# A two-layer decoder step: zero matmuls around the norms, and finer steps in the recurrent branch and the retention output

## The chip, the cores and the metric

One core of a Trainium2 chip. Times are device microseconds of the kernel's execution on that core, in several runs; the profile is that of one execution. TensorE (PE) multiplies, PEld is its weight load, VectorE is DVE, ScalarE is ACT, GpSimd is POOL, and SyncE (SP) issues most DMAs.

## What is computed

Two layers over 256 prompt tokens and 8 x 8 sample tokens (320 in all), model width 1024, f32. Cut to what matters:

```python
for l in range(DEPTH):                                   # DEPTH = 2
    xn = rmsnorm(x, norm1_g[l])
    q, k, v, g_ret, xr, g_rnn, ga, gb = split(xn @ w_in[l])
    o = groupnorm(retention(rotary(q), rotary(k), v, r0[l]))
    ret_out = (silu(g_ret) * o) @ w_ret_out[l]
    xc = conv_b + sum(xcat[:, w:w + t] * cw[w] for w in range(4))      # causal, 4 taps
    r, i = sigmoid(xc @ wa + ba), sigmoid(xc @ wx + bx)                # 16 blocks of 64
    a = exp(-8 * r * softplus(-lam))
    h = scan(a, sqrt(1 - a * a) * i * xc, h0)                          # h_t = a_t h_(t-1) + u_t
    rnn_out = (h * gelu(g_rnn)) @ w_rnn_out[l]
    x = x + (sigmoid(ga) * ret_out + sigmoid(gb) * rnn_out) @ w_o[l]
    x = x + peer(rmsnorm(x, norm2_g[l]), ...)            # top-16 of 128 x 128 experts, 8 heads
y = rmsnorm(x, normf_g)
```

## The kernel before

**Blocks.** All weights of a layer's projections are cut into blocks of 128x1024 (512 KB). `run` (line 222) executes them in a fixed order, one after the other on TensorE. In a layer, counted from 0: 0 to 7 q and k, 8 to 15 v, 16 to 23 `g_ret`, 24 to 31 `xr`, 32 to 39 `g_rnn`, 40 to 47 `ga`, 48 to 55 `gb`, then the two output projections in turn, `w_o`, and the query weights of the expert stage; behind these the expert stage runs its own phases. For f32 accuracy every product is made of three matmuls, so activations and weights are kept as a high and a low part: a block against 320 tokens is 24 matmuls of 320 columns. The blocks 0 and 1 run as one interleaved pair.

**Weight splits.** At the start of block k, `run` calls `split(k + 2)` (its high half is a cast on ScalarE, line 217; its low half a subtraction on VectorE, line 219, or on GpSimd where the block's `lo` says so) and issues the load of block k + 5 on SP. High and low halves have three buffers each.

**Background.** Retention, the recurrent branch (`rglru`) and others are Python generators. `run` advances them by half a block's budget twice in each block, in the middle and at its end; each `yield x` costs x of the budget. The numbers behind `yield` therefore fix at which half block each step's instructions are put into the engines' queues. ScalarE, VectorE and GpSimd execute their queues in order.

**Norms.** `norm_T` (line 157), called before block 0 (`norm1`) and before the query weights (`norm2`) in each layer: squares of x (line 140 on ScalarE, 142 on VectorE; in the first norm here, in the others by the code that made x), the factor r by `rstd` (lines 148 to 154), 24 transposes of x on TensorE into the eight PSUM banks (line 174; x[2] holds the sample tokens and goes first), six matmuls that spread r over partitions (line 178), its copy R, then in eight parts y = x g R (line 191, VectorE), its high part `xh` (193, ScalarE) and its low part `xl` (196, VectorE for parts 0, 3 and 6, else GpSimd). The pair's first matmul (336) waits for the first `xh`. Behind the query pair stand the score matmuls (881), whose keys an SP transfer (872) brings into a pool that is opened after the norm's own is closed.

**Retention output.** Behind retention, `o` is multiplied by the gate in two halves of 1280 elements (671), each cast to `rin_h` (672), with the low parts `rin_l` (678) one step behind.

**Recurrent branch** (`rglru`). For each of 8 channel blocks: `conv(c)` on VectorE (one line 713 and three of line 715), as soon as enough `xr` blocks are done; two gates (728: two f32 matmuls each of 344 columns; 729, tanh on ScalarE) and 731. The convolution runs two blocks ahead of the gates. Then exp (738), Dt in halves (739), one square root over all (741), the state in halves (745 to 748) with eight scans (751), and the branch's output in halves (766, 770, cast 771, low part 772). `bg.drain()` before the first output block forces what is left.

Of the kernel before, what the change touches and what calls it, by code (L numbers as in the profile page):

```python
# [10 lines left out]
F32 = mybir.dt.float32  # L11
F32R = mybir.dt.float32r
F16 = mybir.dt.float16
# [4 lines left out]
OP = mybir.AluOpType  # L18
# [68 lines left out]
class Trunk:  # L87
# [23 lines left out]
    def consts(self):  # L111
        nc, a = self.nc, self.a
        self.ident = self.cp.tile([128, 128], F32, name="ident")
        self.iota_a = self.cp.tile([128, 128, 2], F16, name="iota_a")
        self.gt = self.cp.tile([128, self.depth, 2, 8], F32, name="gt")
        self.eps = self.cp.tile([128, 1], F32, name="eps")
        nc.vector.memset(self.eps, EPS)
        self.nk = self.cp.tile([128, 4, 3], F32, name="nk")
        nc.vector.memset(self.nk, 1.0)
        self.warm()  # L120
        self.x = [self.cp.tile([128, D], F32, name=f"x{t}") for t in range(3)]
        nc.sync.dma_start(self.x[2][:NST], a["x_sample"].rearrange("b t d -> (b t) d"))
        nc.sync.dma_start(self.ident, a["c_ident"])
        for t in range(2):
            nc.sync.dma_start(self.x[t], a["x_prompt"][0, t * 128:(t + 1) * 128, :])
        nc.sync.dma_start(self.gt, a["gt"])
# [18 lines left out]
    def rstd(self, c=slice(0, 3)):  # L145
# [8 lines left out]
        nc.vector.scalar_tensor_tensor(r, w, 1.5, r, op0=OP.add, op1=OP.mult)  # L154
        return self.nk[:, 2, :]

    def norm_T(self, l, which, first=False):
        nc = self.nc
        np_ = self.open("np")
        if first:  # L160
            for k in range(RAWS):
                self.load(k)
            self.late_consts()
            for t in (2, 0, 1):
                for h in range(2):
                    self.square(t, h, np_.tile([128, 512], F32, tag="junk", name="junk", bufs=2), eng=("act", "dve")[h])
        r = self.rstd()
        if first:
            self.split(0)
        ps = [self.bank("acc") for _ in range(4)] + [self.bank("m") for _ in range(2)] + [self.bank("h") for _ in range(2)]  # L170
        for t in (2, 0, 1):
            r0, n = TOK[t]
            for c in range(8):
                nc.tensor.transpose(ps[c][:, r0:r0 + n], self.x[t][:n, c * 128:(c + 1) * 128], self.ident[:n, :n])
        at = {0: (6, NT), 1: (7, NT), 2: (7, NT + 128)}
        for t, (r0, n) in enumerate(TOK):
            b, o = at[t]
            nc.tensor.matmul(ps[b][:, o:o + n], r[:n, t:t + 1].to_broadcast([n, 128]), self.ident[:n, :n], start=True,
                             stop=True, skip_group_check=True)
        R = np_.tile([128, NT], F32, name="R")  # L180
        nc.scalar.copy(R[:, :128], ps[6][:, NT:NT + 128])
        nc.vector.tensor_copy(R[:, 128:], ps[7][:, NT:NT + 192])
        if first:
            self.split(1)
        self.xh = self.cp.tile([128, 8, NT], F32R, tag="xh", name="xh")
        self.xl = self.cp.tile([128, 8, NT], F32R, tag="xl", name="xl")
        ys = {}
        for c in range(9):
            if c < 8:
                ys[c] = y = np_.tile([128, NT], F32, tag="y", name="y", bufs=8)  # L190
                nc.vector.scalar_tensor_tensor(y, ps[c][:, :NT], self.gt[:, l, which, c:c + 1], R, op0=OP.mult,
                                               op1=OP.mult)
                nc.scalar.copy(self.xh[:, c], y)
            if c:
                eng = nc.vector if c - 1 in (0, 3, 6) else nc.gpsimd
                eng.tensor_tensor(self.xl[:, c - 1], ys.pop(c - 1), self.xh[:, c - 1].bitcast(F32), op=OP.subtract)
        self.close("np")
# [24 lines left out]
    def run(self):  # L222
        self.items, self.blocks, self.raw, self.hl = [], [], {}, {}
        for l in range(self.depth):
            Layer(self, l).plan()
        self.credit = self.credit2 = 0.0
        for k, it in enumerate(self.items):
            self.k = k
            if it.get("pre"):
# [41 lines left out]
class Layer:  # L271
# [244 lines left out]
    def retention(self):  # L516
# [148 lines left out]
        while not self.sg_done:  # L665
            yield 0.5
        hi = mx.tile([128, 8, NT], F32R, tag="s3", name="rin_h")
        for j in range(3):
            s = slice(4 * j, 4 * j + 4)
            if j < 2:  # L670
                nc.vector.scalar_tensor_tensor(o[:, s], o[:, s], 0.5, self.sg[:, s], op0=OP.mult, op1=OP.mult)
                nc.scalar.copy(hi[:, s], o[:, s])
                yield 1.5
            if j == 1:
                lo = mx.tile([128, 8, NT], F32R, tag="s1", name="rin_l")
            if j:
                s = slice(4 * j - 4, 4 * j)
                nc.vector.tensor_tensor(lo[:, s], o[:, s], hi[:, s].bitcast(F32), op=OP.subtract)
                yield 1.5
        self.rin = (hi, lo)  # L680
        T.close("rt")
        rg = self.rg = T.open("rg")
# [13 lines left out]
    def rglru(self):  # L696
# [18 lines left out]
                nc.vector.scalar_tensor_tensor(B[:, c, :], A[:, c, w:w + OUTW], vec[:, c, 1 + w:2 + w], B[:, c, :],  # L715
                                               op0=OP.mult, op1=OP.add)

        for c in range(-2, 8):
            if c < 6:
                while self.xr_done < c + 3:  # L720
                    yield 0.5
                conv(c + 2)
            if c < 0:
                yield 1.8
                continue
            for g, dst in ((0, E), (1, Dt)):
                p = T.bank("m")
# [1 line left out]
                nc.scalar.activation(dst[:, c, :], p[:, :OUTW], AF.Tanh, bias=self.hb[:, c, g:g + 1],  # L729
                                     scale=0.5)  # L730
            nc.scalar.activation(C[:, c, :], E[:, c, :], AF.Tanh, bias=z5[:, c:c + 1], scale=z5[:, c:c + 1])
            yield 1.8
        for j in range(2):
            s = slice(4 * j, 4 * j + 4)
            while not self.ge_done:
                yield 0.5
            for c in range(4 * j, 4 * j + 4):
                nc.scalar.activation(E[:, c, :], E[:, c, :], AF.Exp, bias=z6[:, c:c + 1], scale=z6[:, c:c + 1])
            nc.vector.scalar_tensor_tensor(Dt[:, s], Dt[:, s], 1.0, B[:, s], op0=OP.add, op1=OP.mult)
            yield 3.0  # L740
        nc.scalar.activation(C, C, AF.Sqrt, scale=0.25)
        yield 3.5
        for j in range(2):
            s = slice(4 * j, 4 * j + 4)
            nc.vector.tensor_tensor(Dt[:, s], Dt[:, s], C[:, s], op=OP.mult)
            nc.vector.scalar_tensor_tensor(Dt[:, s], E[:, s], 1.0, Dt[:, s], op0=OP.add, op1=OP.mult)
            nc.vector.memset(E[:, s, SEG - 1::3 + DS], 0.0)
            nc.vector.tensor_copy(Dt[:, s, SEG - 1::3 + DS], self.h0[:, s, :])
            yield 3.0
            for c in range(4 * j, 4 * j + 4):  # L750
                nc.vector.tensor_tensor_scan(B[:, c, :], E[:, c, :], Dt[:, c, :], 0.0, op0=OP.mult, op1=OP.add)
                if c % 2:
                    yield 0.9
        nc.scalar.copy(rec[:, :, 9:12], A[:, :, SEG - 3:SEG])
        nc.scalar.copy(rec[:, :, 12:36].rearrange("p c (b w) -> p c b w", w=3), seg[:, :, :, DS:DS + 3])
        nc.scalar.copy(rec[:, :, 0:1], B[:, :, NPT - 1:NPT])
# [4 lines left out]
        ge = self.ge  # L761
        hi = rg.tile([128, 8, NT], F32R, tag="C", name="hin_h")
        lo = rg.tile([128, 8, NT], F32R, tag="D", name="hin_l")
        for j in range(2):
            s = slice(4 * j, 4 * j + 4)
            nc.vector.tensor_tensor(ge[:, s, :NPT], ge[:, s, :NPT], B[:, s, :NPT], op=OP.mult)
            for c in range(4 * j, 4 * j + 4):
                bs = bass_seg(B[:, c, :])
                gs = ge[:, c, NPT:].rearrange("p (b t) -> p b t", t=DS)
                nc.vector.tensor_tensor(gs, gs, bs, op=OP.mult)  # L770
            nc.scalar.copy(hi[:, s], ge[:, s])
            nc.vector.tensor_tensor(lo[:, s], ge[:, s], hi[:, s].bitcast(F32), op=OP.subtract)
            yield 3.0
        self.hin = (hi, lo)

    def post_rnn(self, c):
# [648 lines left out]
```

## Time and profile before

| | |
|---|---|
| runs (us) | 2508.48, 2512.42, 2505.75; median 2508.48 |
| profiled execution | 2508.14, of which the span from the first to the last instruction is 2506.4 |
| mean granted TensorE clock | 0.985 |
| busy share of the span | PE 97%, PEld 87%, DVE 78%, ACT 44%, POOL 19% |
| matmuls | 16556 |
| idle of TensorE for a weight's low half | 12.6 + 8.4 us in its two longest groups |

A busy share is an average over stages with different limits: TensorE is never far from full, so what is to be read is where it waits, and at which clock it goes on afterwards. In the rows, the number in square brackets is the idle time of the engine ahead of the row and what ended it; the granted clock is given as a share of 2.4 GHz. A layer takes some 1250 us; times are counted from the span's start, and the second layer's first norm lies near 1250.

### The profile page before, as it was taken

The numbers are of one execution on the slowest core, as the hardware profiler recorded it, in microseconds if no ns is written. First come the engines' busy times: TensorE is split into PE (matmuls) and PEld (weight loads), VectorE is DVE, ScalarE is ACT, GpSimd is POOL, SyncE is SP. The second block draws the span as 40 slices with busy tenths as digits, with TensorE's granted clock in tenths as the row PEclk, the third lists the DMA queues.
The fourth block names the chain that finished last, engine by engine and source line by source line (L and its number), as shares of the span: only waits on it lengthen the run. The fifth ranks groups of instructions, "written<-read, shape, count | busy, mean of one in ns | idle before, by whom it ended". The sixth has DMA issues, their size and how long they took to land. (4 is left out here: it accounts for less than half of the span.)

```text
span 2506.4 us, 42676 instructions
## 1 busy us (share of the span) xinstructions
PE 2419.1 (97%) x16556; PEld 2175.8 (87%) x16556; DVE 1943.1 (78%) x3491; ACT 1092.6 (44%) x1539; POOL 485.4 (19%) x305
## 2 busy tenths in 40 slices
PE   8999999999999999999999899999998999999998
PEld 7879898999898897688788798999998988976886
DVE  7465657888788878989864656578887988788897
ACT  4336434455334443244544373444543344432444
POOL 0000003100102541145300000041001035411453
PEclk9999999999999999999999899999999999999999
DMA  6333444456867998899752334444568689988996
GB/s 235 117 110 118 130 151 130 149 177 227 306 202 275 355 352 303 289 335 355 287 206 89 109 113 142 143 132 156 184 233 294 203 295 351 350 309 291 328 356 238
DMA packets 174507, 571.67 MB, mean 228 GB/s; under 512 B 20832, under 2 KB 28000, under 8 KB 173536
## 3 DMA queue, kind: packets, MB, share of 16 engines
q1 hardware_dynamic: 135568, 427.54, 50.1%
q0 software_dynamic: 36864, 134.23, 14.0%
q10 hardware_dynamic: 1872, 7.16, 0.8%
q8 instruction: 130, 2.13, 0.3%
q14 instruction: 73, 0.60, 0.1%
HBM read 545.76 MB, written 23.10 MB: 227 GB/s over the span
## 5 line engine op out<-in xcount | busy, mean ns | idle before, releaser
L217 ACT CAST hi<-raw 128x1024 fp32r<-128x1024 f32 x684 | 717.0, 1049 | 686.9 <-PE ps_acc L1199 393.4
L219 DVE TENSOR_TENSOR lo<-raw,hi 128x1024 fp32r<-128x1024 f32 x660 | 803.2, 1221 | 270.1 <-ACT hi L217 267.2
L945 PE MATMUL ps_h<-xh,lo 128*128 128x256 f32 x2048 | 582.8, 285 | 12.6 <-DVE lo L219 12.6
L943 PE MATMUL ps_h<-xh,hi 128*128 128x256 f32 x2048 | 587.8, 287 | 0.0
L944 PE MATMUL ps_h<-xl,hi 128*128 128x256 f32 x2048 | 581.6, 284 | 0.0
L945 PEld LDWEIGHTS ps_h<-xh,lo 128*128 128x128 f32 x2048 | 395.1, 193 | 14.7 <-DVE lo L219 14.5
L944 PEld LDWEIGHTS ps_h<-xl,hi 128*128 128x128 f32 x2048 | 395.5, 193 | 0.1
L943 PEld LDWEIGHTS ps_h<-xh,hi 128*128 128x128 f32 x2048 | 395.3, 193 | 0.1
L1197 PE MATMUL ps_acc<-hi,hh 128*128 128x512 f32 x944 | 373.8, 396 | 0.0
L1198 PE MATMUL ps_acc<-lo,hh 128*128 128x512 f32 x944 | 368.4, 390 | 2.7 <-DVE lo L219 2.7
L1199 PE MATMUL ps_acc<-hi,hl 128*128 128x512 f32 x944 | 369.0, 391 | 0.7
L1243 POOL DMA_INDIRECT g<-in_peer_u,eS x128 | 203.4, 1589 | 781.8 <-DVE g L1252 490.1
L356 PE MATMUL ps_acc<-xh,hi 128*128 128x320 f32 x960 | 310.6, 324 | 3.0 <-ACT hi L217 3.0
L358 PE MATMUL ps_acc<-xh,lo 128*128 128x320 f32 x960 | 301.8, 314 | 8.4 <-DVE lo L219 8.4
L357 PE MATMUL ps_acc<-xl,hi 128*128 128x320 f32 x960 | 300.4, 313 | 0.0
L1243 POOL DMA_INDIRECT g<-in_peer_v,eS x128 | 203.0, 1586 | 349.5 <-DVE xs L1266 286.9
L1198 PEld LDWEIGHTS ps_acc<-lo,hh 128*128 128x128 f32 x944 | 177.4, 188 | 41.7 <-DVE lo L219 5.3
L1199 PEld LDWEIGHTS ps_acc<-hi,hl 128*128 128x128 f32 x944 | 177.2, 188 | 41.3 <-DVE hl L1167 4.4
L1197 PEld LDWEIGHTS ps_acc<-hi,hh 128*128 128x128 f32 x944 | 177.3, 188 | 36.1 <-issue 1.4
L358 PEld LDWEIGHTS ps_acc<-xh,lo 128*128 128x128 f32 x960 | 183.7, 191 | 11.2 <-DVE lo L219 11.0
L356 PEld LDWEIGHTS ps_acc<-xh,hi 128*128 128x128 f32 x960 | 183.9, 192 | 10.3 <-ACT hi L217 5.0
L1252 DVE SCALAR_TENSOR_TENSOR g<-g,xs 128x1024 f32<-128x1024 f32 x128 | 156.4, 1222 | 46.0 <-DMA g<-in_peer_u,eS 44.8
(284 smaller groups left out, 3369.5 us busy)
## 6 DMA issues: line engine op xcount, KB each, us to landing
raw<-in_ut SPq DMA_DIRECT2D x256, 512.0 KB
raw<-in_peer_v SPq DMA_DIRECT2D x256, 512.0 KB
raw<-in_wall SPq DMA_DIRECT2D x192, 512.0 KB
sA<-kept SPq DMA_DIRECT2D x96, 256.0 KB
kept<-sA SPq DMA_DIRECT2D x64, 256.0 KB
r<-in_r0t SPq DMA_DIRECT2D x2, 2048.0 KB
out_sr_s<-r ACTq DMA_DIRECT2D x2, 2048.0 KB
aux<-in_c_mP SPq DMA_DIRECT2D x16, 192.0 KB
```

The lines of the kernel that those rows point to most:

```text
L217: nc.scalar.copy(hi, raw)
L219: eng.tensor_tensor(lo, raw, hi.bitcast(F32), op=OP.subtract)
L356: nc.tensor.matmul(o, wh, xh[:, k, :], start=k == 0, stop=False)
L357: nc.tensor.matmul(o, wh, xl[:, k, :], start=False, stop=False)
L358: nc.tensor.matmul(o, wl, xh[:, k, :], start=False, stop=k == 7)
L943: nc.tensor.matmul(o, uh, xh, start=k == 0, stop=False, skip_group_check=True)
L944: nc.tensor.matmul(o, uh, xl, start=False, stop=False, skip_group_check=True)
L945: nc.tensor.matmul(o, ul, xh, start=False, stop=k == 7, skip_group_check=True)
L1197: nc.tensor.matmul(self.acc[t][d], hh[:, s], hi[:, c], start=first, stop=False)
L1198: nc.tensor.matmul(self.acc[t][d], hh[:, s], lo[:, c], start=False, stop=False)
L1199: nc.tensor.matmul(self.acc[t][d], hl[:, s], hi[:, c], start=False, stop=last)
L1243: nc.gpsimd.indirect_dma_start(out=g, out_offset=None, in_=T.a[tab].rearrange("l e d -> (l e) d"), in_offset=bass.IndirectOffsetOnAxis(ap= ...
```

## The change

A tile of zeros `fill` (128x256, f16) is written by GpSimd at the start. `keep_clock` issues matmuls of it into a PSUM bank, whose result nothing reads. In each of the four calls of `norm_T` it does so: ten of 256 columns ahead of all transposes (16 in the first), four of 192 ahead of the transposes of x[0] and four ahead of those of x[1], sixteen of 192 behind the matmuls that spread r. In the first norm, block 0 is split between the squares of x[0] and x[1] instead of behind `rstd`, and block 1's low half goes to GpSimd. The retention output goes in quarters, all high parts first. The convolution runs three blocks ahead; the steps of the recurrent branch are cut finer, with other numbers behind `yield`.

```diff
+    def keep_clock(self, out, n):
+        for _ in range(n):
+            self.nc.tensor.matmul(out, self.fill[:, :128], self.fill[:, :out.shape[1]], start=True, stop=True,
+                                  skip_group_check=True)
...
                     self.square(t, h, np_.tile([128, 512], F32, tag="junk", name="junk", bufs=2), eng=("act", "dve")[h])
+                if t == 0:
+                    self.split(0)
         r = self.rstd()
-        if first:
-            self.split(0)
+        self.keep_clock(self.bank("m")[:, :256], 16 if first else 10)
...
         for t in (2, 0, 1):
             r0, n = TOK[t]
+            if t < 2:
+                self.keep_clock(ps[6][:, NT:NT + 192], 4)
...
+        self.keep_clock(ps[5][:, NT:NT + 192], 16)
         R = np_.tile([128, NT], F32, name="R")
...
+        self.items[1]["lo"] = "pool"
...
-        for j in range(3):
-            s = slice(4 * j, 4 * j + 4)
-            if j < 2:
-                nc.vector.scalar_tensor_tensor(o[:, s], o[:, s], 0.5, self.sg[:, s], op0=OP.mult, op1=OP.mult)
-                nc.scalar.copy(hi[:, s], o[:, s])
-                yield 1.5
...
+        parts = [slice(2 * j, 2 * j + 2) for j in range(4)]
+        for s in parts:
+            nc.vector.scalar_tensor_tensor(o[:, s], o[:, s], 0.5, self.sg[:, s], op0=OP.mult, op1=OP.mult)
+            nc.scalar.copy(hi[:, s], o[:, s])
+            yield 0.8
+        lo = mx.tile([128, 8, NT], F32R, tag="s1", name="rin_l")
+        for s in parts:
+            nc.vector.tensor_tensor(lo[:, s], o[:, s], hi[:, s].bitcast(F32), op=OP.subtract)
+            yield 0.8
...
-        for c in range(-2, 8):
-            if c < 6:
-                while self.xr_done < c + 3:
+        for c in range(-3, 8):
+            if c < 5:
+                while self.xr_done < c + 4:
                     yield 0.5
-                conv(c + 2)
+                conv(c + 3)
             if c < 0:
-                yield 1.8
+                yield 2.3
                 continue
...
-            yield 1.8
+            yield 2.3 if c < 5 else 0.8
...
-            nc.vector.scalar_tensor_tensor(Dt[:, s], Dt[:, s], 1.0, B[:, s], op0=OP.add, op1=OP.mult)
-            yield 3.0
+            for c in range(4 * j, 4 * j + 4, 2):
+                c2 = slice(c, c + 2)
+                nc.vector.scalar_tensor_tensor(Dt[:, c2], Dt[:, c2], 1.0, B[:, c2], op0=OP.add, op1=OP.mult)
+                yield 1.2
         nc.scalar.activation(C, C, AF.Sqrt, scale=0.25)
         yield 3.5
-        for j in range(2):
-            s = slice(4 * j, 4 * j + 4)
+        for j in range(4):
+            s = slice(2 * j, 2 * j + 2)
             nc.vector.tensor_tensor(Dt[:, s], Dt[:, s], C[:, s], op=OP.mult)
...
-            yield 3.0
-            for c in range(4 * j, 4 * j + 4):
+            yield 2.0
+            for c in range(2 * j, 2 * j + 2):
                 nc.vector.tensor_tensor_scan(B[:, c, :], E[:, c, :], Dt[:, c, :], 0.0, op0=OP.mult, op1=OP.add)
-                if c % 2:
-                    yield 0.9
+                yield 0.85
...
-        for j in range(2):
-            s = slice(4 * j, 4 * j + 4)
+        for j in range(4):
+            s = slice(2 * j, 2 * j + 2)
             nc.vector.tensor_tensor(ge[:, s, :NPT], ge[:, s, :NPT], B[:, s, :NPT], op=OP.mult)
...
-            yield 3.0
+            yield 2.2
```

The queue of VectorE in the first norm, first before and then changed (lines 142 and 144 are the squares, of x[2], x[0] and x[1] in this order; 219 and 230 the low half of a weight block, here of block 0 and 1):

```order
L142 SCALAR_TENSOR_TENSOR junk,nk<-x_78 64x512
L142 SCALAR_TENSOR_TENSOR junk,nk<-x_76 128x512
L142 SCALAR_TENSOR_TENSOR junk,nk<-x_77 128x512
L148 TENSOR_TENSOR nk<-nk 128x3
L150 TENSOR_SCALAR nk<-nk 128x3
L151 RECIPROCAL nk<-nk 128x3
L152 SCALAR_TENSOR_TENSOR nk<-nk 128x3
L153 TENSOR_TENSOR nk<-nk 128x3
L154 SCALAR_TENSOR_TENSOR nk<-nk 128x3
L219 TENSOR_TENSOR lo<-raw,hi 128x1024
L182 COPY R<-ps_h 128x192
L219 TENSOR_TENSOR lo<-raw,hi 128x1024
```

```order
L144 SCALAR_TENSOR_TENSOR junk,nk<-x_80 64x512
L144 SCALAR_TENSOR_TENSOR junk,nk<-x_78 128x512
L230 TENSOR_TENSOR lo<-raw,hi 128x1024
L144 SCALAR_TENSOR_TENSOR junk,nk<-x_79 128x512
L150 TENSOR_TENSOR nk<-nk 128x3
L152 TENSOR_SCALAR nk<-nk 128x3
L153 RECIPROCAL nk<-nk 128x3
L154 SCALAR_TENSOR_TENSOR nk<-nk 128x3
L155 TENSOR_TENSOR nk<-nk 128x3
L156 SCALAR_TENSOR_TENSOR nk<-nk 128x3
L193 COPY R<-ps_h 128x192
L202 SCALAR_TENSOR_TENSOR y<-ps_acc,gt,R 128x320 x2
```

The split of block 0 moved ahead of the last square, and the split of block 1 left this queue.

The queue of ScalarE in the retention tail, before and changed (217 and 228 cast a weight block; 497 and 498, now 509 and 510, take over an `xr` block from TensorE; 729 and 738 are the tanh of the first gates):

```order
L217 CAST hi<-raw 128x1024
L497 COPY xcat<-ps_acc 128x256
L498 COPY xcat<-ps_acc 128x8x8
L703 COPY xcat<-cbuf 128x8x8x3
L217 CAST hi<-raw 128x1024
L497 COPY xcat<-ps_acc 128x256
L498 COPY xcat<-ps_acc 128x8x8
L729 ACTIVATE rg_a<-ps_m,hb 128x344
L729 ACTIVATE rg_i<-ps_m,hb 128x344
```

```order
L712 COPY xcat<-cbuf 128x8x8x3
L228 CAST hi<-raw 128x1024
L509 COPY xcat<-ps_acc 128x256
L510 COPY xcat<-ps_acc 128x8x8
L228 CAST hi<-raw 128x1024
L509 COPY xcat<-ps_acc 128x256
L510 COPY xcat<-ps_acc 128x8x8
L738 ACTIVATE rg_a<-ps_m,hb 128x344
L738 ACTIVATE rg_i<-ps_m,hb 128x344
```

One more weight block (a cast and the take-over of an `xr` block) now stands between the start of the recurrent branch and its first gates.

The queue of ScalarE around the square root, before (lines 217, 694, 741) and changed (228, 703, 752); 694 and 703 take over the `ga` blocks:

```order
L217 CAST hi<-raw 128x1024
L694 ACTIVATE sgate_1686<-ps_acc 128x320
L217 CAST hi<-raw 128x1024
L741 ACT_TABLE_LOAD
L741 ACTIVATE rg_r<-rg_r 128x2752
L694 ACT_TABLE_LOAD
L694 ACTIVATE sgate_1686<-ps_acc 128x320
```

```order
L228 CAST hi<-raw 128x1024
L703 ACTIVATE sgate_1735<-ps_acc 128x320
L752 ACT_TABLE_LOAD
L752 ACTIVATE rg_r<-rg_r 128x2752
L228 CAST hi<-raw 128x1024
L703 ACT_TABLE_LOAD
L703 ACTIVATE sgate_1735<-ps_acc 128x320
```

The square root moved ahead of one cast of a weight block.

## Rows read from the trace of the kernel before

**Rows 1.** The waits of TensorE: us in total, times, longest us
```profile
PE ps_m L728 <- DVE xc L715: 8.2, 2, 4.1
```

**Rows 2.** Timeline of TensorE, retention tail: start, us, what, idle before
```profile
188.29 2.66 PE L728 MATMUL ps_m<-xc,gw 128*128 128x344 f32 x4 [4.09 <-DVE xc L715]
190.24 0.97 PE L356 MATMUL ps_acc<-xh,hi 128*128 128x320 f32 x1
...
193.72 1.32 PE L728 MATMUL ps_m<-xc,gw 128*128 128x344 f32 x4
194.62 0.57 PE L356 MATMUL ps_acc<-xh,hi 128*128 128x320 f32 x1
...
196.64 0.74 PE L728 MATMUL ps_m<-xc,gw 128*128 128x344 f32 x2
```

**Rows 3.** Window of 2.5 us there: busy and count by engine, clock
```profile
190.00:192.50 2.50, 2.50 (x9) 2.09 (x8) 2.39 (x5) 1.90 (x4) 0.00 (x0) 0.50 0.62 210
```

**Rows 4.** Timeline of VectorE, retention tail of layer 0, the first convolution
```profile
186.43 1.80 DVE L715 SCALAR_TENSOR_TENSOR xc<-xcat,vec,xc 128x344 f32<-128x344 f32 x3
```

**Rows 5.** Windows of 20 us: tail of the recurrent branch, retention in either layer
```profile
160.00:180.00 20.00, 20.00 (x130) 18.10 (x129) 11.63 (x26) 5.56 (x10) 0.00 (x0) 1.00 0.42 163
240.00:260.00 20.00, 19.28 (x131) 18.95 (x131) 13.21 (x13) 15.76 (x20) 0.00 (x0) 1.00 0.38 123
260.00:280.00 20.00, 16.25 (x104) 14.94 (x102) 17.23 (x26) 6.91 (x12) 0.00 (x0) 1.00 0.36 122
280.00:300.00 20.00, 18.75 (x115) 18.49 (x116) 8.95 (x8) 8.39 (x13) 0.00 (x0) 0.91 0.49 158
300.00:320.00 20.00, 20.00 (x138) 20.00 (x137) 11.26 (x18) 7.87 (x11) 0.00 (x0) 1.00 0.42 132
1400.00:1420.00 20.00, 20.00 (x104) 17.60 (x103) 11.03 (x34) 2.86 (x6) 0.00 (x0) 0.79 0.16 53
```

**Rows 6.** Timeline of ScalarE and VectorE, tail of the recurrent branch, layer 0
```profile
246.64 2.50 ACT L741 ACTIVATE rg_r<-rg_r 128x2752 f32<-128x2752 f32 x1
...
273.49 1.49 DVE L772 TENSOR_TENSOR hin_l<-ge,hin_h 128x1280 fp32r<-128x1280 f32 x1 [1.33 <-ACT hin_h L771]
...
280.54 3.63 DVE L219 TENSOR_TENSOR lo<-raw,hi 128x1024 fp32r<-128x1024 f32 x3
```

**Rows 7.** Timeline of the first norm of layer 0
```profile
9.28 0.16 DVE L148 TENSOR_TENSOR nk<-nk 128x3 f32<-128x3 f32 x1
...
9.89 1.04 ACT L217 CAST hi<-raw 128x1024 fp32r<-128x1024 f32 x1
...
10.63 1.84 PE L178 MATMUL ps_h<-ident,nk 128*128 128x128 f32 x6
```

**Rows 8.** Groups of GpSimd: count, busy us, mean ns, idle before
```profile
L219 POOL TENSOR_TENSOR lo<-raw,hi 128x1024 fp32r<-128x1024 f32 x24 | 57.6, 2399 | 53.7 <-ACT hi L217 53.7
```

**Rows 9.** Window over sixteen f16 matmuls of 64 columns (lines 1117, 1118)
```profile
1990.85:1991.36 0.51, 0.47 (x16) 0.47 (x17) 0.51 (x1) 0.00 (x0) 0.00 (x0) 1.00 0.96 169
```

**Rows 10.** Timeline of the second norm of layer 0
```profile
390.02 0.66 PE L174 MATMUL ps_acc<-ident,x 128*128 128x128 f32 x4
...
391.97 1.07 PE L178 MATMUL ps_h<-ident,nk 128*128 128x128 f32 x6
...
394.65 0.51 PE L336 MATMUL ps_acc<-xh,hi 128*128 128x320 f32 x1 [1.61 <-ACT xh L193]
...
400.40 0.33 SPq L872 DMA_DIRECT2D H<-in_keyst  x1
...
404.71 0.68 PE L881 MATMUL ps_m<-H 128*128 128x128 f32 x4 [1.16 <-ACT hi L217]
```

**Rows 11.** Window over the start of the pair behind that norm
```profile
395.00:397.50 2.50, 2.50 (x11) 2.35 (x11) 2.43 (x6) 1.42 (x4) 2.18 (x3) 0.50 0.00 0
```

**Rows 12.** Timeline of TensorE, first norm of layer 1
```profile
1251.63 1.11 PE L174 MATMUL ps_acc<-ident,x 128*128 128x128 f32 x4
...
1255.04 0.97 PE L178 MATMUL ps_h<-ident,nk 128*128 128x128 f32 x6
```

More of the change, by code (lines that the diff above doesn't have):

```diff
@@ L117, in consts @@
         nc.vector.memset(self.eps, EPS)
+        self.fill = self.cp.tile([128, 256], F16, name="fill")
+        nc.gpsimd.memset(self.fill, 0.0)
         self.nk = self.cp.tile([128, 4, 3], F32, name="nk")
@@ L667, in retention @@
         hi = mx.tile([128, 8, NT], F32R, tag="s3", name="rin_h")
-        for j in range(3):
-            s = slice(4 * j, 4 * j + 4)
-            if j < 2:
-                nc.vector.scalar_tensor_tensor(o[:, s], o[:, s], 0.5, self.sg[:, s], op0=OP.mult, op1=OP.mult)
-                nc.scalar.copy(hi[:, s], o[:, s])
-                yield 1.5
[L674 to L679, printed above, removed]
+        parts = [slice(2 * j, 2 * j + 2) for j in range(4)]
[7 more added lines that the diff above has]
+            yield 0.8
         self.rin = (hi, lo)
@@ L763, in rglru @@
         lo = rg.tile([128, 8, NT], F32R, tag="D", name="hin_l")
-        for j in range(2):
-            s = slice(4 * j, 4 * j + 4)
+        for j in range(4):
+            s = slice(2 * j, 2 * j + 2)
             nc.vector.tensor_tensor(ge[:, s, :NPT], ge[:, s, :NPT], B[:, s, :NPT], op=OP.mult)
-            for c in range(4 * j, 4 * j + 4):
+            for c in range(2 * j, 2 * j + 2):
                 bs = bass_seg(B[:, c, :])
```

## Prediction

> **What bounds the kernel.** I read the page first: TensorE is busy 97% of the span, VectorE 78%, so the time is TensorE's work plus its gaps and the stretches at half clock. The mean granted clock is 0.985, so both together are small, and the view to read is TensorE's waits. Their fifth-largest line is the one this change aims at: the gate matmuls of the recurrent branch (line 728) wait twice, once in each layer, 4.1 us each time, for the convolution on VectorE [rows 1]. The timeline shows what follows such a wait: the four gate matmuls start at 188.29 after 4.09 us of idle, twelve weight-block matmuls run from 190.24 to 193.72, the next gates from 193.72 to 194.62, and the next twelve matmuls from 194.62 to 196.64 [rows 2]. In between the granted clock is 0.50, that is 1.2 instead of 2.4 GHz [rows 3]. The convolution ends at 186.43 + 1.80 = 188.23 [rows 4], so it ends the wait. A second weak stretch shows in windows of 20 us: TensorE starts 138 matmuls in an undisturbed one (0.145 us each), but 131, 104 and 115 in the three before it [rows 5]. The norms are the third place.
>
> **Retention tail, both layers.** The loss before is 4.09 of idle; the first gates take 1.95 (188.29 to 190.24) where the next take 0.90, so 1.05 more; twelve matmuls take 3.48 where the next twelve take 2.02, 1.46 more [rows 2]. Together 6.6 us. The change lets the convolution run three blocks ahead and so puts the first gates behind the whole weight block 30. That block is 24 matmuls, 24 x 0.145 = 3.5 us, which lies where the idle was. VectorE's own work stays the same and is still a closed row of instructions (the quarter steps cost only the fixed part of four more of them), so the first convolution still ends near 188.2. Block 30 runs from 184.0 to 187.5; then the gates wait 0.75. The next two gates still follow 12 matmuls apart (0.9 + 1.75 = 2.65 us, with the drain between them some 2.9), while a convolution with the weight split that VectorE has between two of them takes 0.46 + 1.80 + 1.22 = 3.5: walked in order they come 0.5 and 0.4 late. These 1.65 us remain, each wait too short, I take it, for the clock to fall (a choice: only the 4.1 us wait shows the fall here). Gain 6.6 - 1.65 = **4.95 a layer, 9.9 in all**. Bounds: 6.6 with no wait left; 3 if the second and third wait are twice as long and the first one is followed by half clock. The cover for block 30 is thin: its low half must be ready at 184.0, and by the queue it is done 0.4 earlier.
>
> **Tail of the recurrent branch, both layers.** Against 138 matmuls, 7 + 34 + 23 = 64 are missing in 60 us, 64 x 0.145 = 9.3 us [rows 5]. VectorE is the cause: it has about 20 us of the recurrence to do besides the weight splits, and it stands still twice for 1.33 while ScalarE casts half of the branch's output; the three splits at 280.54 stand in a heap behind it [rows 6], and the clock falls once more (0.91 over the window 280 to 300). The change starts the state steps earlier and spreads them over eight blocks instead of six. I walked both queues in the new order with the old durations. The square root (2.50 us [rows 6] and its table load, 1.28) now stands ahead of the cast of block 44 instead of behind it, which makes that split 1.25 late. Blocks 50 to 53 are then late by 0.1, 1.65, 0.25 and 2.8, since eight blocks of 3.5 us are 28 and VectorE needs 20 + 8 x 1.2 and what it waits for ScalarE. Sum 6.05. Gain 9.3 - 6.05 = 3.25, **6.5 in both layers**. Bounds: 0 (the wait moves entirely to the splits) to 6 (the quarters overlap without idle and no half clock is left).
>
> **The first norm.** Weight block 0 lands late: its cast starts at 9.89 as soon as it is there [rows 7], when the squares of x1 are long done. Both engines take instructions in order, so with the split put ahead of the square of x1, the square waits for the block: cast to 10.94, low half on VectorE to 12.2, square and its sum 0.77, the chain to the factor r 1.3 (from 9.28 to the spreading at 10.63 before), 14.3. The matmuls that spread r start at 14.35 instead of 10.63 [rows 7], 3.7 later. What comes back: VectorE has neither split between r and the scaled output any more, 2 x 1.22 (3.63 for three [rows 6]), so the pair starts 3.7 - 2.4 = 1.3 later. Block 1's low half goes to GpSimd at 2.40 [rows 8], is ready near 18.7, and the fifth matmul of the pair needs it; the high half follows R, so this holds up 44 of the pair's 48 matmuls a little more, 0.2 by my walk. Sum: **-1.5**, bounds -3.5 (the whole delay of r) to -0.5 (the pair at full clock). The first 16 fillers and the eight between the transposes cost nothing here: r comes at 14.3, and the transposes were done before 10.63 [rows 7]; if r stayed early, they would cost up to 3 us.
>
> **The second norms.** A filler costs 0.03 us per 64 columns (16 matmuls of 64 columns in 0.51 us [rows 9]), so 0.09 for 192 and 0.12 for 256 columns, double at half clock. Ten of 256 lie in waits for x. The eight of 192 before the transposes of x0 and x1 are on the path: r is ready as the transposes end, and the spreading starts at 391.97 [rows 10]. 8 x 0.09 = 0.7. The sixteen behind it, 16 x 0.09 = 1.4, fit into the 1.61 us that the pair waits for its first cast [rows 10]. What they might give back is the half clock in the pair: the granted clock is 0.50 in the whole window from 395 to 397.5 [rows 11]; half of that is 1.25, with the edges some 1.45 us. But behind the pair TensorE stands 1.16 us for the keys, whose transfer is issued at 400.40, once GpSimd has written its last low half [rows 10]; the pair's own speed doesn't move that; layer 1 is taken alike. So **-0.7 each, -1.4 in all**; bounds -1.4 (fillers at half clock) to +0.8 each.
> The Trainium skill (TensorE: Matmul & The Clock Gate, Part 1) says that the throttled state is the default and that activity releases it, so fillers that keep TensorE fed would save the half-clock stretch. The trace agrees that the stretch follows the idle. By that page both second norms and the first would each gain about 1.5, and the sum would be 4.5 us lower; the rows put the key's wait in the way.
>
> **The first norm of layer 1.** Here even the transposes run at half clock: four take 1.11 against 0.66 in the second norm, and from the first of x0 to the spreading it is 3.41 us (1251.63 to 1255.04) against 1.95 [rows 10, 12]. At full clock that saves 1.46, less 0.7 of fillers; I take the pair behind it to lose the same 1.45 as the pair of the second norm, and nothing waits for keys there: **+2.2**, bounds -1.4 (half clock all the same, and fillers at double price) to +2.5.
>
> **Sum.** 9.9 + 6.5 - 1.5 - 1.4 + 2.2 = 15.7. The profiled execution took 2508.14 us, 0.3 below the median of the three runs; 2508.1 - 15.7 = **2492.4**. About 0.3%, 7.5 us, is what a measurement of this kernel can tell from no change.
>
> **The rivals.** *VectorE is the bound in the long tail as well, or the clock falls elsewhere.* For it: the 20 us of recurrence are not made smaller, only cut. Against it: two blocks more to spread them over. Without the 6.5 the time is 2498.9. In layer 1 TensorE started only 104 matmuls from 1400 to 1420 at clock 0.79, where layer 0's 160 to 180 had 130 at 1.00 [rows 5], with the same program: which of the two a run gets is open, and 6 us more or less; with it in both layers 2505. Chance 0.24.
> *The second norms and the first gain from the clock as well.* The row of the wait behind the pair names ScalarE's cast as its releaser [rows 10], not the keys; if that is so, a pair at full clock brings everything behind it forward by the 1.45 of half clock: three times 1.5, 2492.4 - 4.5 = 2488. It is the case in which the rule quoted above holds to the end. Against it: that cast ended before TensorE went on only by chance of the order, as nothing of it enters the score matmuls. Chance 0.12.
> *One halt becomes two (slower).* Place: the low half of block 30, or of 31, which VectorE now has between the quarters of the retention output and three convolutions. If it is later than the end of block 29 (184.0) by about the 2.3 us of one convolution, TensorE stands there and again at the first gates, with half clock behind both. Price: a halt cost 6.6, so each layer loses 6.6 more instead of gaining 4.95; with the norms -1.5, -1.4 and -1.4 and the long tail 6.5 it is -13.2 - 4.3 + 6.5 = -11: 2519. For it: VectorE's row is closed from 184 to 200; against it: the split is 0.4 early by the walk. Chance 0.12.
> *The forecast*, 0.52, has 2485 to 2500 as its own range (both tails at their better or worse bounds by half).
>
> **How the numbers follow.** The range 2483 to 2506 takes in the forecast, the first two rivals and leaves out the third, and the corners where both tails give all or nothing: some 0.2. Faster by more than 0.3% is under 2500.6: nearly all of the forecast (0.51), the fillers (0.12) and a third of the first rival (0.07), 0.70. Slower than 2515.7 is the last rival, 0.12; the rest 0.18.
>
> **What would show it.** Right: gates behind block 30 with under 1 us of wait and a granted clock of 1.00 from 187 to 193; the matmuls of 240 to 300 at 105 or more in each window; the pair of the first norm ending at 25 to 26; the wait for keys as long as before. Wrong: a wait of a weight-block matmul for a split in the retention tail; idle in the long tail of the old length under other names; granted 0.50 in the pair of layer 1's first norm in spite of the fillers; a first norm that gets its r at 10.6 as before.

## The result, and the profile after

The changed kernel took 2493.35 us in the median of four runs (2492.47 to 2496.84), the kernel before 2509.8 (2505.75 to 2512.42): ratio 0.9941, 95% interval 0.9922 to 0.9961, so 16 us or 0.6% faster. The forecast was 2492.4. The profiled execution is the slowest of the four; its page begins

```profile
span 2495.0 us, 42998 instructions
...
PE 2421.3 (97%) x16698; PEld 2174.4 (87%) x16698; DVE 1947.2 (78%) x3526; ACT 1094.0 (44%) x1547; POOL 485.4 (19%) x307
```

The span fell from 2506.4 to 2495.0, by 11.3 us before rounding, less than the medians' 16.5. Where it fell is read from the rows in which ScalarE takes a block's result over from TensorE, the same work in both kernels. Of layer 0, before: the first `xr` block, the last `g_rnn` block, the first `ga` and the last `gb` block.

```profile
160.39 0.37 ACT L497 COPY xcat<-ps_acc 128x256 f32<-128x256 f32 x1 [5.67 <-PE ps_acc L358]
...
235.47 0.44 ACT L690 ACTIVATE ge<-ps_acc 128x320 f32<-128x320 f32 x1 [2.15 <-PE ps_acc L358]
...
240.43 0.43 ACT L694 ACTIVATE sgate<-ps_acc 128x320 f32<-128x320 f32 x1
...
300.95 0.44 ACT L694 ACTIVATE sgate<-ps_acc 128x320 f32<-128x320 f32 x1 [2.15 <-PE ps_acc L358]
```

The same four take-overs after the change:

```profile
163.00 0.37 ACT L509 COPY xcat<-ps_acc 128x256 f32<-128x256 f32 x1 [5.67 <-PE ps_acc L370]
...
232.82 0.44 ACT L699 ACTIVATE ge<-ps_acc 128x320 f32<-128x320 f32 x1 [2.15 <-PE ps_acc L370]
...
237.78 0.42 ACT L703 ACTIVATE sgate<-ps_acc 128x320 f32<-128x320 f32 x1
...
294.79 0.44 ACT L703 ACTIVATE sgate<-ps_acc 128x320 f32<-128x320 f32 x1 [2.15 <-PE ps_acc L370]
```

From the first to the second row is the retention tail, 75.08 before and 69.82 after; from the third to the fourth the long tail of the recurrent branch, 60.52 and 57.01. All places read in this way (first norm: from the start to the first take-over of q; second norm: from the last matmul ahead of it to the first score matmul; layer 1's first norm: from the last matmul ahead of it to the first take-over of q), each with the gain that was forecast:

| place | forecast | before | after | gain |
|---|---|---|---|---|
| first norm | -1.5 | 23.66 | 26.30 | -2.6 |
| retention tail, layer 0 | 4.95 | 75.08 | 69.82 | 5.3 |
| long tail, layer 0 | 3.25 | 60.52 | 57.01 | 3.5 |
| second norm, layer 0 | -0.7 | 17.44 | 16.92 | 0.5 |
| first norm, layer 1 | 2.2 | 17.59 | 15.19 | 2.4 |
| retention tail, layer 1 | 4.95 | 75.34 | 69.83 | 5.5 |
| long tail, layer 1 | 3.25 | 60.54 | 58.56 | 2.0 |
| second norm, layer 1 | -0.7 | 16.54 | 16.92 | -0.4 |
| sum | 15.7 | | | 16.2 |

What is missing to 11.3 lies in the two expert stages, where the program is the same: from the first score matmul to the next norm 844.0 before and 847.5 after, and in layer 1, to the end, 853.7 and 855.0. That is 4.8 us that the change has no part in.

The waits of TensorE in the changed kernel that answer to [rows 1] and to the norms:

```profile
PE ps_h L188 <- DVE nk L156: 3.1, 1, 3.1
PE ps_m L891 <- ACT hi L228: 3.0, 2, 1.5
...
PE ps_m L737 <- DVE xc L724: 1.6, 6, 0.3
```

The gates (now line 737) wait six times, 1.6 us in all, instead of twice 4.1. The timeline and two windows (the second lies in the second norm) answer to [rows 2, 3, 11]:

```profile
190.66 1.43 PE L737 MATMUL ps_m<-xc,gw 128*128 128x344 f32 x4 [0.33 <-DVE xc L724]
...
194.09 1.39 PE L737 MATMUL ps_m<-xc,gw 128*128 128x344 f32 x4 [0.25 <-DVE xc L724]
...
197.44 1.39 PE L737 MATMUL ps_m<-xc,gw 128*128 128x344 f32 x4 [0.19 <-DVE xc L724]
```

```profile
190.00:192.50 2.50, 2.17 (x11) 1.51 (x10) 2.44 (x4) 1.42 (x4) 0.00 (x0) 1.00 0.00 0
389.00:391.50 2.50, 2.50 (x15) 2.13 (x16) 2.44 (x5) 1.66 (x4) 1.97 (x3) 1.00 0.00 0
```

Gates behind block 30, waits of 0.33, 0.25 and 0.19, granted clock 1.00 where it was 0.50.

The first norm, answering to [rows 7]:

```profile
9.72 1.05 ACT L228 CAST hi<-raw 128x1024 fp32r<-128x1024 f32 x1 [1.83 <-DMA raw<-in_wall]
...
10.67 0.62 ACT L142 ACTIVATE junk<-x 128x512 f32<-128x512 f32 x1
...
14.09 1.84 PE L188 MATMUL ps_h<-ident,nk 128*128 128x128 f32 x6 [3.11 <-DVE nk L156]
...
15.86 2.74 PE L161 MATMUL ps_m<-fill 128*128 128x192 f16 x16
...
16.21 2.35 POOL L230 TENSOR_TENSOR lo<-raw,hi 128x1024 fp32r<-128x1024 f32 x1 [15.16 <-ACT hi L228]
...
18.31 0.62 PE L348 MATMUL ps_acc<-xh,hi 128*128 128x320 f32 x1
```

The square of x1 waits for block 0's cast, the spreading (188) starts at 14.09 as forecast. But the pair (348) starts at 18.31, not near 16.3. Sixteen fillers stand in front of it from 15.86, at half clock, 0.15 us each: the fillers ahead had ended before the 3.11 us of idle, and the clock fell there. They are not the whole delay. In the kernel before, VectorE's copy of the spread r waited for TensorE, when the low half of block 0 was long done (10.97 + 1.23 = 12.20). And without any filler (the run no_fill below) the pair follows the spreading after 3.31 us:

```profile
12.50 0.36 DVE L182 COPY R<-ps_h 128x192 f32<-128x192 f32 x1 [0.31 <-PE ps_h L178]
```

```profile
13.78 1.72 PE L185 MATMUL ps_h<-ident,nk 128*128 128x128 f32 x6 [3.38 <-DVE nk L156]
17.09 0.63 PE L344 MATMUL ps_acc<-xh,hi 128*128 128x320 f32 x1 [1.59 <-ACT xh L200]
```

With the fillers it is 4.22 us (14.09 to 18.31), so they delay the pair by 0.9; before it was 4.37 (10.63 to 15.00), so taking the splits away gave 1.1.

The second norm of layer 0 and the first of layer 1, answering to [rows 10, 12]:

```profile
386.29 0.97 PE L188 MATMUL ps_h<-ident,nk 128*128 128x128 f32 x6
...
388.87 0.41 PE L348 MATMUL ps_acc<-xh,hi 128*128 128x320 f32 x1 [0.18 <-ACT xh L204]
...
394.63 0.33 SPq L882 DMA_DIRECT2D H<-in_keyst  x1
...
398.04 0.68 PE L891 MATMUL ps_m<-H 128*128 128x128 f32 x4 [1.48 <-ACT hi L228]
```

```profile
1248.77 0.60 PE L184 MATMUL ps_acc<-ident,x 128*128 128x128 f32 x4
...
1250.85 0.97 PE L188 MATMUL ps_h<-ident,nk 128*128 128x128 f32 x6
...
1253.43 0.42 PE L348 MATMUL ps_acc<-xh,hi 128*128 128x320 f32 x1 [0.18 <-ACT xh L204]
```

In the second norm the pair follows at full clock, and TensorE then stands 1.48 us for the keys instead of 1.16: what the pair gained is waited away. The row names ScalarE's cast, which here ended within 0.1 us of the key transfer. That it is the transfer is seen where the two lie apart, as in bridge (a run below), whose score matmul (890) starts while the cast runs:

```profile
406.36 1.05 ACT L224 CAST hi<-raw 128x1024 fp32r<-128x1024 f32 x1
...
406.98 0.68 PE L890 MATMUL ps_m<-H 128*128 128x128 f32 x4 [0.54 <-DMA H<-in_keyst]
```

In layer 1's first norm four transposes take 0.60 instead of 1.11.

### The profile page after: what moved, and what is told of

It is laid out like the page before. It is cut to its first block, busy times and chain, and to the rows that moved or that the text cites. A ratio compares the mean times of both kernels' runs of the same rounds, so it can differ in the third digit from the quotient of the medians.

```text
span 2495.0 us, 42998 instructions
## 1 busy us (share of the span) xinstructions
PE 2421.3 (97%) x16698; PEld 2174.4 (87%) x16698; DVE 1947.2 (78%) x3526; ACT 1094.0 (44%) x1547; POOL 485.4 (19%) x307
## 5 line engine op out<-in xcount | busy, mean ns | idle before, releaser
L963 ACT ACTIVATE H<-ps_h 128x512 f32<-128x512 f32 x128 | 76.5, 597 | 256.4 <-PE ps_h L955 256.3
```

## The experiments

Durations below are of the places of the table. A kernel that was executed once is told by its places, since whole times scatter by several us; whole times are given where there are several executions.

**The tails alone, the norms alone, the fillers, the first norm's order.** Base of the first, third and fourth is the changed kernel, of the second the kernel before. Edits (tails_only has both edits shown, no_fill the first, first_old the second; norms_only has the norms as changed and all else as before):

```diff
-        self.keep_clock(self.bank("m")[:, :256], 16 if first else 10)
...
-            if t < 2:
-                self.keep_clock(ps[6][:, NT:NT + 192], 4)
...
-        self.keep_clock(ps[5][:, NT:NT + 192], 16)
```

```diff
-                if t == 0:
-                    self.split(0)
         r = self.rstd()
+        if first:
+            self.split(0)
...
-        self.items[1]["lo"] = "pool"
```

> The changed kernel without any filler and with the first norm as before; retention output, convolution and recurrent branch stay as changed. Theory (the two tails are worth some 16 us, the norms together about nothing): 5.3 + 3.5 in layer 0 and 5.5 + 2.0 in layer 1 from the two profiles, so about 2509.8 - 16 = 2493.5, equal to the changed kernel within 3 us; its profile has block 39's take-over some 5 us and block 55's some 9 us earlier than before in layer 0. Rival (the fillers do it, the clock is what counts): more than 6 us slower than the changed kernel, over 2499.

> The kernel before with the fillers and with the first norm as changed; the tails as before. Theory: +2.6 in the first norm, -0.5 and +0.4 in the second norms, -2.4 in layer 1's first norm, in all 0 within 3 us of before, 2507 to 2513. Rival (clock): 6 us or more faster than before, under 2504.

> The changed kernel without fillers, the first norm's order as changed. Theory: the first pair starts 1.3 us earlier than with fillers, near 17.0, since sixteen fillers at half clock stood in front of it, but it runs at half clock; layer 1's first norm gives back its 2.4; second norms within 0.5. Total 2494 to 2497. Rival (fillers are worth the half clock of all four norms, 1.45 each): 2499 or more.

> The changed kernel with block 0's split behind the factor r as before and block 1's low half on VectorE, fillers kept. Theory: the factor r comes at 10.6 instead of 14.1, unless the fillers between the transposes hold the spreading up; the pair starts near 15 to 16 and what follows is 2 to 3 us earlier than in the changed kernel: 2490.5 to 2491.5. Rival (it is the pair's feeding by VectorE that counts, the split's place gives nothing): within 0.5 us of the changed kernel at the first take-over of q (26.3).

Measured against 2508.36 us of the kernel before (19 runs): tails_only 2497.77, ratio 0.9952 (0.9926 to 0.9978); norms_only 2510.34, 1.0008 (0.9989 to 1.0027); no_fill 2498.95, 0.9962 (0.9947 to 0.9977); first_old 2489.82, 0.9931 (0.9904 to 0.9959). The tails bring most of the gain: tails_only lies between theory and rival by its median, but its places are as forecast, 57.02 in both long tails, 69.82 in the retention tail of layer 1 (72.46 in layer 0, where the clock stood at half from 152 to 173). The norms in sum bring nothing, as norms_only's theory had it. The median of no_fill lies between its theory and its rival, and its interval overlaps that of the changed kernel, so what the fillers are worth is read from the places alone. The fillers and the order of the first norm are two opposite things in that sum. At the first take-over of q:

| kind of first norm | without fillers | with fillers |
|---|---|---|
| old order | 23.66, 23.85, 23.79 | 21.45, 22.25, 21.80 |
| new order | 27.69 | 26.30, 25.31, and 25.1 to 26.3 in four more kernels |

(Before, tails_only, bridge; first_old, joined and pool_only, in which only the split is in the old place; no_fill; the changed kernel, norms_only.) So the fillers give some 2 us here, and the new order takes 3 to 5; first_old gained more at this place (4.85 us) than its theory's 2 to 3. The theory of no_fill was right on the start of the pair (17.09), wrong on what follows: without fillers the half clock lasts until 24.2, in the changed kernel until 20.6, so the fillers gain more than the 0.9 by which they delay the pair. Layer 1's first norm took 15.19 to 15.21 with all fillers (nine kernels) and 15.90, 15.97, 17.58 and 17.59 without (no_fill, tails_only, bridge, before): 0.7, and 2.4 where half clock hits the transposes. In the second norms the kernels with all fillers took 16.55 to 17.88, 17.1 in the mean of 18 values, those without 16.32 to 18.12, 17.1 in the mean of 8: neither gain nor loss.

The first norm with the old order and fillers:

```profile
9.27 1.04 ACT L228 CAST hi<-raw 128x1024 fp32r<-128x1024 f32 x1
...
10.16 1.07 PE L188 MATMUL ps_h<-ident,nk 128*128 128x128 f32 x6 [1.11 <-DVE nk L156]
...
14.16 0.41 PE L347 MATMUL ps_acc<-xh,hi 128*128 128x320 f32 x1 [1.50 <-ACT xh L204]
```

Block 0's cast no longer stands in front of a square; the spreading starts at 10.16 after 1.11 us of idle instead of 3.11, and the pair at 14.16; the granted clock is 1.00 from 8 to 24.

**Which half of the first norm's edit costs.** Only the split goes back, block 1's low half stays on GpSimd:

> The changed kernel with block 0's split behind the factor r as before; block 1's low half stays on GpSimd, fillers stay. Read at the first take-over of q: before 23.7, changed 25.1 to 26.3 in its runs, with both edits undone 21.45. Theory (the square that waits for block 0 costs the 3.5 us, GpSimd's low half little): 21.4 to 22.2, the spreading near 10.2. Rival (GpSimd's low half is what the pair waits for): 24 or more.

```profile
10.47 1.07 PE L188 MATMUL ps_h<-ident,nk 128*128 128x128 f32 x6
...
12.29 2.36 POOL L230 TENSOR_TENSOR lo<-raw,hi 128x1024 fp32r<-128x1024 f32 x1 [11.23 <-ACT hi L228]
```

First take-over of q at 21.80: theory. Moving the split back gave 3.3 to 4.5 us (25.12 to 26.32 in the kernels with the new order and fillers); GpSimd's low half costs nothing that can be told (21.45 and 22.25 with VectorE's).

**What makes the retention tail shorter.** lead_two puts the lead back to two with its yields (first edit), halves the retention output (second):

```diff
-        for c in range(-3, 8):
-            if c < 5:
-                while self.xr_done < c + 4:
+        for c in range(-2, 8):
+            if c < 6:
+                while self.xr_done < c + 3:
...
-                conv(c + 3)
+                conv(c + 2)
```

```diff
-        parts = [slice(2 * j, 2 * j + 2) for j in range(4)]
...
+        for j in range(3):
+            s = slice(4 * j, 4 * j + 4)
```

> The changed kernel with the convolution two blocks ahead and its yields as before; quarters and finer states stay. Read in each layer from the first xr take-over to the last g_rnn take-over: before 75.1 and 75.3 us, changed 69.8 in both. Theory (the three blocks of lead put block 30 under the convolution's delay): 74 to 75.5, with a wait of 3.5 us or more for the first gates and half clock behind it. Rival (the finer quarter steps free VectorE earlier): 71 or less.

> The changed kernel with the retention output in two halves and its yields as before; the lead of three stays. Same stage. Theory: within 1 us of the changed kernel, 69.3 to 70.8; the low half of block 30 may come up to 0.7 late because a half step of 1.49 us stands ahead of it. Rival (the quarters carry the gain): 74 or more.

With a lead of two the stage takes 74.96 and 75.01 us in the two layers, with halves 69.64 in both, 0.2 less than with quarters. It is the lead, with the yields that belong to it; the quarters cost a little. The first gates of lead_two, and a window behind them:

```profile
189.47 2.66 PE L737 MATMUL ps_m<-xc,gw 128*128 128x344 f32 x4 [3.85 <-DVE xc L724]
...
190.00:192.50 2.50, 2.50 (x7) 1.59 (x6) 2.39 (x5) 0.88 (x2) 0.00 (x0) 0.50 0.32 88
```

A wait of 3.85 and then half clock, as before. The lead's edit does not end with this stage, though: the long tail of lead_two takes 55.51 and 55.50 us, 1.5 less than the changed kernel's 57.01. Of the 5.1 us that the edit gives in the retention tail, 1.5 are lost again in the long one; why is seen below.

**What the half clock is worth.** In the kernel before:

```diff
+            if c == 0:
+                T.keep_clock(T.bank("m")[:, :256], 36)
             for g, dst in ((0, E), (1, Dt)):
```

> The kernel before with 36 fillers of 256 columns directly ahead of the first gates in each layer, all else as before; they cover the 4.1 us of idle with work that nobody reads. Theory (6.6 us a layer are 4.1 of waiting for the convolution and 2.5 of half clock behind it): the stage from the first xr to the last g_rnn take-over goes from 75.1 to 72.3 to 73 us, the first gates start within 0.3 us of 4.2 us behind the block and the granted clock is 1.00 there. Rival (the clock fall has another cause than that idle): 75 or more.

```profile
190.20 4.10 PE L161 MATMUL ps_m<-fill 128*128 128x256 f16 x36
194.44 1.42 PE L737 MATMUL ps_m<-xc,gw 128*128 128x344 f32 x4
...
195.00:197.50 2.50, 2.50 (x15) 2.06 (x14) 2.39 (x5) 2.14 (x4) 0.00 (x0) 1.00 0.33 74
```

The stage takes 73.16 us in both layers instead of 75.08 and 75.34, a little above the theory's 73; the gates start 4.2 us behind the first filler, so the wait itself has stayed, and go on at granted clock 1.00 instead of 0.50. So of the loss of a retention tail about 2 us are half clock and 4.1 the wait itself. The Trainium skill (TensorE: Matmul & The Clock Gate, Part 1) says that activity releases the throttle. The trace agrees, with matmuls of zeros as the activity: the granted clock is 1.00 behind them.

**The long tail.** old_states takes the steps behind the gates back to halves; spread_out changes three numbers:

```diff
-                yield 1.2
+                yield 1.5
         nc.scalar.activation(C, C, AF.Sqrt, scale=0.25)
...
-            yield 2.0
+            yield 1.8
...
-            yield 2.2
+            yield 2.5
```

> The changed kernel with the recurrent branch behind the gates (exp, Dt, square root, states, branch output) in the old halves and yields. Read from the first to the last take-over of the gate blocks: before 60.5 in both layers, changed 57.0, or 58.6 where the clock fell. Theory: 60 to 61, and the retention tail keeps its 69.8. Rival (the tail got shorter because the retention tail in front of it did): 57 to 58.

> The changed kernel with three numbers behind yields: 1.5 for 1.2 (the square root goes behind a cast again, as before), 1.8 for 2.0 and 2.5 for 2.2 (a weight split stands between all four parts of the branch's output, where the last two had none between). First to last take-over of the gate blocks: changed 57.0. Theory (0.8 us of its 5.0 us of idle come from the square root ahead of the cast, some 1.5 from the two last parts in one heap): 54.6 to 55.6 in both layers where the clock does not fall. Rival (VectorE's work as a whole is the bound, the order gives nothing): 56.8 to 57.5.

old_states took 58.99 in both layers, which neither side had forecast; bridge, with the old steps too, has 58.99 in layer 0. In both the clock did not fall there, whereas in the profile before it fell in both layers (60.52, 60.54). So the finer steps are worth 2.0 us a layer behind a lead of three, and 1.5 of the 3.5 in the table are the clock, which fell in layer 1 before and after, so that its gain is the bare 2.0; behind a lead of two they are worth 3.5 (58.99 in bridge, 55.51 in lead_two). spread_out took 54.97 in both: theory. What it removed is seen in the changed kernel's end of the tail, on TensorE and on VectorE (782 is the low part of the branch's output, 776 and 780 its products, 230 a weight's low half):

```profile
282.96 0.41 PE L368 MATMUL ps_acc<-xh,hi 128*128 128x320 f32 x1 [1.59 <-ACT hi L228]
...
284.22 0.41 PE L370 MATMUL ps_acc<-xh,lo 128*128 128x320 f32 x1 [0.70 <-DVE lo L230]
```

```profile
279.50 0.82 DVE L782 TENSOR_TENSOR hin_l<-ge,hin_h 128x640 fp32r<-128x640 f32 x1 [0.80 <-ACT hin_h L781]
280.25 0.68 DVE L776 TENSOR_TENSOR ge<-ge,xc 128x512 f32<-128x512 f32 x1
280.85 0.35 DVE L780 TENSOR_TENSOR ge<-ge,xc 128x64 f32<-128x64 f32 x2
281.99 0.83 DVE L782 TENSOR_TENSOR hin_l<-ge,hin_h 128x640 fp32r<-128x640 f32 x1 [0.79 <-ACT hin_h L781]
282.94 3.77 DVE L230 TENSOR_TENSOR lo<-raw,hi 128x1024 fp32r<-128x1024 f32 x3
```

The fourth part starts right behind the third, without a weight split between, and three splits follow in a heap; TensorE waits for ScalarE's cast, which waits for a buffer, and then for the low half, 2.6 us in all between starts. In spread_out a split stands there:

```profile
281.42 0.83 DVE L782 TENSOR_TENSOR hin_l<-ge,hin_h 128x640 fp32r<-128x640 f32 x1 [0.80 <-ACT hin_h L781]
282.37 1.23 DVE L230 TENSOR_TENSOR lo<-raw,hi 128x1024 fp32r<-128x1024 f32 x1
283.52 0.69 DVE L776 TENSOR_TENSOR ge<-ge,xc 128x512 f32<-128x512 f32 x1
```

So it does in lead_two, which has the changed kernel's 1.2, 2.0 and 2.2. It was thus the edit of the lead, with its yields, that moved the fourth part ahead of the split and cost the 1.5 us:

```profile
284.73 1.23 DVE L230 TENSOR_TENSOR lo<-raw,hi 128x1024 fp32r<-128x1024 f32 x1 [0.45 <-ACT hi L228]
285.87 0.69 DVE L776 TENSOR_TENSOR ge<-ge,xc 128x512 f32<-128x512 f32 x1
```

**Together.** joined is the changed kernel with the first norm's old order, halves, and the three numbers; joined_no_mid has no fillers between the transposes either.

> What the runs so far speak for, together: the changed kernel with the first norm's order as before (4.9 us earlier at the first take-over of q), the retention output in halves (0.2 a layer), and the three numbers of the run before (some 2 a layer). Theory: the kernel with the first norm's order alone stood at 2489.8 us; less 0.4 and less 4: 2485 to 2487. Rival (the gains of one place are lost at the next): 2489 to 2492.

> The same without the four fillers ahead of the transposes of x[0] and of x[1] in each norm. Theory (8 x 0.09 us on the path in three norms, nothing in the first, and those behind the spreading alone keep the clock): 0.7 us less from the last matmul ahead of a norm to its first pair, 1.5 to 2 us in all. Rival (they keep the clock up in the transposes): a norm with transposes at half clock, and no gain or up to 3 us of loss.

Against 2509.18 us (11 runs): joined 2485.41 (2480.19 to 2490.66), ratio 0.9902 (0.9875 to 0.993); joined_no_mid 2487.64 (2482.81 to 2493.88), 0.9908 (0.988 to 0.9936). joined is the fastest kernel here by its median, 1% under the one before; its interval overlaps that of the changed kernel by a little. It overlaps that of first_old by more, so it is the places that show the gains to add up: its retention tails are 69.64, its long tails 55.10, its first take-over of q is at 22.25. In the one profile of joined_no_mid no transposes run at half clock, so nothing shows that the fillers between them do anything for the clock; they cost 0.6 us in layer 1's first norm (15.21 and 14.58). The 1.5 to 2 us of the theory are below what whole times can tell, and layer 1's second norm was the longest of all there (18.68), since TensorE waited 3.6 us for transfers. A lead of two together with the three numbers was not tried.

## Why the prediction was right

**Retention tail** (forecast 4.95, measured 5.3 and 5.5): right in mechanism and size. Block 30 filled the wait, and lead_two takes the gain back whole. Two terms were too large, and their errors nearly cancel: the remaining waits were 0.33, 0.25 and 0.19, 0.8 in sum instead of 1.65, and the 6.6 of loss were 6.1 by bridge, 4.1 of wait and some 2 of half clock instead of 2.5. 6.1 - 0.8 is the 5.3. (The wait aimed at is the fourth line of TensorE's waits, not the fifth; nothing hangs on it.)

**Long tail** (3.25; measured 3.5 and 2.0): the walk of the new order was right. It had 1.25 at the square root and then 0.1, 1.65, 0.25 and 2.8; the profile has starts that are late by 0.8 at the square root and then by 1.4, 0.2 and 2.6, five in all against 6.05. The term mis-sized is the loss before, 9.3: it was 3.5 + 5.0 = 8.5, and 1.5 of that was half clock that the old steps don't always cost. The finer steps by themselves are worth 2.0 here. That the lead's edit would cost 1.5 in this tail was not foreseen.

**First norm** (-1.5; measured -2.6): the delay of the spreading was right (14.35, measured 14.09), and so was GpSimd (18.7, measured 16.21 + 2.35 = 18.56). The step that failed is "the pair starts 3.7 - 2.4 = 1.3 later": it started 3.3 later. The 2.4 were 1.1, since only block 1's split had stood between r and the scaled output; block 0's had ended while VectorE still waited for the spreading (12.50). And the fillers behind the spreading, which the prediction left out here though it had considered them at half clock for the second norms, delayed the pair by 0.9.

**Second norms** (-0.7 each; measured +0.5 and -0.4): the eight fillers cost 0.5 rather than 0.7 (4.70 us before and 5.17 after from the last matmul to the spreading), and the wait for the keys took the pair's gain. The prediction took layer 1 to be like layer 0, but there the score matmuls had waited 0.08 us before, and 1.48 after. The +0.5 of layer 0 came from the keys themselves, used 3.41 us behind their issue at 394.63 where it was 4.31 before; over all kernels the fillers give and take nothing here. The rival by which the pair's clock counts is out for this norm: its clock was 1.00 and the wait grew.

**First norm of layer 1** (2.2; measured 2.4): right against the profile before; against kernels whose transposes happened not to run at half clock the fillers give 0.7.

**The rivals.** One halt becoming two did not come: in the retention tail no weight block waited for a split. The clock in retention was, as said, open: a long stretch of half clock in layer 1's retention stood in both profiles (0.79 in [rows 5]; from 1389 to 1403 after). It costs 6.1 us: from the first take-over of q to that of `xr` it took 142.8 us, in layer 0 of the same profiles 136.7. Such a stretch was found in layer 1 of spread_out too, in layer 0 of tails_only and bridge, and in neither layer of the nine others, some of which have shorter ones.

That the whole came out within 1 us of the forecast is partly luck: the first norm was forecast 1.1 too good, the other places 1.6 too bad, and the expert stages alone scatter by several us.

## What to carry to other kernels

Where the busiest engine waits for a producer, count what follows the wait as well: here TensorE waited 4.1 us and lost some 2 us more behind it, at half clock. Move independent work into the wait, or at least zeros, which kept the clock here (bridge). They cost nothing where they ended before the wait did, and 0.5 to 0.9 us where they stood on the path. In a queue that is executed in order, never put an instruction that waits for a late transfer ahead of a short one that others wait for: here that cost 3.3 to 4.5 us and swallowed what the fillers gave. And read a change by stages, the next one too: its two halves had opposite signs in the same norm, the edit of the lead lost 1.5 us a stage later, and only the runs that separated the edits showed the faster kernel.

## What the runs showed of the hardware that was not expected

The expert stage of layer 0, identical in all kernels, took 844.0 to 852.1 us from the first score matmul to the next norm in fourteen profiles, and that of layer 1 853.7 to 861.2: each scatters by half of the change's gain. The keys of the second norms took 3.0 to 5.5 us from their issue to the first score matmul, with the same program behind the norm. The long half clock in the retention stage came and went between executions of kernels with the same retention code, some 6 us each time; what sets it was not tried.
